# Own places for the last query and gate tiles of group two, a split store in the output pairs, and fewer steps at the end of group one's last descending scan tile

## The chip, the cores and the metric

The kernel runs on one core of one Trainium2 chip. A NeuronCore has five engines that run at the same time, each with its own queue of instructions that it takes in order: TensorE (PE, matrix multiplication; the loading of its weights is shown apart as PEld), VectorE (DVE), ScalarE (ACT), GpSimd (POOL) and SyncE (SP), which here does little but start DMA transfers. Engines wait for each other and for transfers by semaphores. The metric is the time of one execution on the device, in microseconds (us); lower is better. It is the median of several executions.

## The reference

One layer of a bidirectional encoder on two request groups with shared weights: 1024 rows of `x_sample` and 256 rows of `x_prompt`, 2048 features each. The layer adds to `x` the product of `w_out` with three groups of heads side by side, all computed from one projection of the normed rows:

```python
hn = rms_norm(x, norm_g)
proj = hn @ w_in
xbc, z_ssd, dt_raw, q, k, v, z_att, mq, z_mem = split_cols(proj, IN_SIZES)
xbc = silu(centred_dwconv(xbc, conv_w, conv_b))
...
y_f = ssd_scan(xs, dt[:, :, 0], A[0], Bm, Cm)                # over the rows, ascending
y_b = ssd_scan(reversed rows, dt[:, ::-1, 1], A[1], ...)     # and descending
yg = (y_f + y_b + d_skip * xs) * silu(z_ssd)
o_ssd = rms_norm(yg in two halves, ssd_norm_g)
o_att = window_attention(rms_norm(q), rms_norm(k), v, sink) * silu(z_att)
o_mem = softmax(rms_norm(mq) @ rms_norm(mk)) @ mv * silu(z_mem)
return x + concat([o_ssd, o_att, o_mem]) @ w_out
```

All of it is float32.

## The kernel before

**Rows and groups.** The 1280 rows are ten tiles of 128. Group one is tiles 0 to 4, group two tiles 5 to 9 (`base` is 0 or 5). Each float32 factor is kept as two parts, a rounded one and the rest (`xH`, `xL` for the rows, `wh`, `wl` for the weights), and each product is three matmuls. ACT writes `wh` (L216) and DVE `wl` (L217) from a loaded weight tile `wraw`.

**Blocks.** The work is a row of weight blocks, one behind the other. `block_tok` takes 512 columns of weights over 16 feature chunks k and five row tiles into five PSUM banks of the tag `acc`; each k is 15 matmuls of 128x512. In the last step (k = 14 and 15 together) the five tiles are finished in turn, and each is evicted by a function: `ev_gate` (ACT takes the tanh at L318, DVE finishes the gate at L319, SP stores it at L320) for the blocks z0 and z1, `ev_raw` (ACT copies at L341, SP stores at L342) for q and mq. `block_feat` computes 256 features of 640 rows with matmuls of 128x320; its last step is 48 matmuls. For group two the order is kv, q, za0, za1, z0, z1, mq, zm0, zm1, and then four output blocks o of 512 columns of `w_out` each. These work on the rows of group one, whose results have been refilled into `xH` and `xL` by then.

**Places.** A tile pool hands out buffers by tag. The evictions use the tags `evu` and `evt`, two buffers each, in turn: tile i takes `evt` for odd i and `evu` for even i, so the third `evu` tile of a block (i = 4) gets the buffer of the first (i = 0) once its store has landed. Only q of group one is different: its tiles 3 and 4 have places of their own (`tL7`, `tH7`). The tag `ch` has four buffers (`CH = 4`) of 128x640; it holds the chunks `chd` that `fill_direct` loads (L188) and splits into `xH` (L197, L200) and `xL` (L198, L201). `refill_o` (L1531) makes such refills during zm1 (at k = 3 and 7) and during the first output block (at k = 1 and 5): the attention outputs, the memory outputs and the two scan outputs `oT` become the rows that the output blocks multiply. Before it does, `need` runs the lane's steps until the tiles that it loads are finished.

**Lanes.** Attention, memory attention and the scan are generators in two queues (lane 0 and lane 1). After each k of a block, `pump` adds a rate to what each lane is owed and runs as many steps as are owed; a step runs a generator to its next `yield`. For group two the rates of lane 1 are 2.75 a feature block's two k's, that is 1.375 a k, in zm, and 2.4 a k in o. A feature block's last four k's come behind its last matmul. In `run`, a refill's `need` comes before the pump of the same k. The build puts each engine's instructions in order from such priorities and its own estimate of when operands are ready, so a load without operands can be issued long before its place in the program.

**The descending scan.** `ssd_down(t)` runs for t = 7 down to 0 in lane 1, then `ssd_up(8)`, `ssd_up(9)`, `ssd_down(9)`, `ssd_down(8)`. Each tile adds its parts, multiplies by the gate, and takes the sum of squares (L1146); POOL makes the factor `yrs` (L1157). `norm_ssd` (DVE, L1074) scales the two halves, and `turn_ssd(g)` turns half g: POOL sets a word (`yw`, L1082), PE transposes into `pr` (L647), ACT copies to `so` (L1088), SP stores to `oT` (L1089). A tile's norm and turns are done in the steps of the next tile; the last tile of a run (t = 0 or 8, `first`) does its own, after some empty steps. `ssd_up` starts with loads (`rf`, `rb`, L922) and has among its steps `xf` (L950), `fh` (L952) and the matmul `pst` (L937).

**The output of group two** comes in eight pairs (`block_pair`, with Strassen-like products over seven PSUM tiles p = 1, 2, 6, 5, 3, 7, 4 in that order, 3 matmuls of 128x320 for each p and k). `ev_pair` adds the seven products into two row blocks `r0` and `r1` (two halves of 320 each) and a helper `w`, all adds on DVE at L1240, and stores them: `r0` whole at L1256, the halves of `r1` at L1259 and L1262.

## Time and profile before

| what | value |
|---|---|
| time, median of 3 executions | 1773.84 us (1771.46 to 1775.32) |
| the profiled execution's own time | 1773.66 us |
| its span, first to last instruction | 1772.0 us |
| PE busy | 1762.2 us, 99% of the span, 11044 matmuls |
| DVE, ACT, POOL busy | 70%, 51%, 31% |
| bytes moved by DMA | 301.16 MB, mean 170 GB/s |
| stores of q, z, mq tiles of group two | 927 to 932, 1071 to 1077, 1149 to 1155, 1221 to 1227 us |
| first output block | from 1311.66 us |
| output pairs | from 1570.76 us |

A row of a timeline has the start in us from the span's start, the duration, the engine (a small q behind it marks its instruction queue, which issues DMAs), the line, the operation, the output and inputs by the program's names, the shape and the count; in square brackets stands how long the engine had been idle, and what ended it. A wait row has who waited, for whom, the total in us, the times and the longest. A row of windows has the stretch, its length, each engine's busy time and count, the granted clock of PE, the share of DMA time and GB/s.

### The profile page before, as it was taken

The page shows a single profiled execution, that of the slowest core. Times are in us where ns is not written, and L with a number is a line of the kernel's source. Part 1 is how long each engine was busy: PE and PEld are TensorE (multiplying, and loading weights), DVE is VectorE, ACT ScalarE, POOL GpSimd, SP SyncE. Part 2 cuts the span into 40 slices and gives each one's busy share as a digit, 9 for nine tenths or more (in the row PEclk, how much of TensorE's full clock was granted, in tenths as well). Part 3 has the DMA queues.
Part 4 walks back from the last instruction along what each step waited for, and adds up shares of the span by engine and source line. Part 5 has one row for each costly group of instructions (what it writes and reads, how often), then busy time and mean ns, then how long its engine had stood idle before and what let it go on. Part 6 is the DMA issues. An engine that isn't in the chain of part 4 may idle for free. (4 is left out here: it accounts for less than half of the span.)

```text
span 1772.0 us, 31942 instructions
## 1 busy us (share of the span) xinstructions
PE 1762.2 (99%) x11044; PEld 1608.4 (91%) x11044; DVE 1246.0 (70%) x2351; ACT 901.6 (51%) x2010; POOL 555.6 (31%) x980
## 2 busy tenths in 40 slices
PE   9999999999999999999999999999999999999999
PEld 7889999999998999999889988888988888899999
DVE  5596788888868878878665676566776654766665
ACT  6555455554434756656454555544446533543332
POOL 0105899998810100001001000011110000058775
PEclk9999999999999999999999999999999999999999
DMA  9654444445446645454545645557777755744442
GB/s 308 189 182 130 136 151 146 144 140 169 124 140 209 197 134 151 140 153 122 186 121 173 201 149 161 172 161 249 225 246 226 257 188 148 218 142 148 145 144 77
DMA packets 208210, 301.16 MB, mean 170 GB/s; under 512 B 19568, under 2 KB 86192, under 8 KB 208048
## 3 DMA queue, kind: packets, MB, share of 16 engines
q1 hardware_dynamic: 207904, 299.06, 54.1%
q8 instruction: 87, 1.43, 0.3%
q14 instruction: 75, 0.61, 0.1%
q10 hardware_dynamic: 144, 0.06, 0.0%
HBM read 236.36 MB, written 62.69 MB: 169 GB/s over the span
## 5 line engine op out<-in xcount | busy, mean ns | idle before, releaser
L217 DVE TENSOR_TENSOR wl<-wraw,wh 128x512 fp32r<-128x512 f32 (+1 forms) x480 | 346.4, 724 | 238.4 <-ACT wh L216 225.4
L216 ACT ACTIVATE wh<-wraw 128x512 fp32r<-128x512 f32 (+1 forms) x480 | 292.2, 613 | 301.6 <-PE acc L270 154.6
L268 PE MATMUL acc<-wh,xH 128*128 128x512 f32 (+1 forms) x1088 | 418.1, 385 | 0.0
L270 PE MATMUL acc<-wh,xL 128*128 128x512 f32 (+1 forms) x1088 | 410.4, 377 | 0.0
L269 PE MATMUL acc<-wl,xH 128*128 128x512 f32 (+1 forms) x1088 | 409.5, 376 | 0.0
L270 PEld LDWEIGHTS acc<-wh,xL 128*128 128x128 f32 x1088 | 204.2, 188 | 37.0 <-issue 0.2
L268 PEld LDWEIGHTS acc<-wh,xH 128*128 128x128 f32 x1088 | 204.3, 188 | 36.5 <-issue 2.7
L269 PEld LDWEIGHTS acc<-wl,xH 128*128 128x128 f32 x1088 | 204.5, 188 | 35.0 <-issue 1.2
L303 PE MATMUL acc<-xH,wh 128*128 128x320 f32 x640 | 203.0, 317 | 0.0
L305 PE MATMUL acc<-xH,wl 128*128 128x320 f32 x640 | 198.8, 311 | 0.0
L304 PE MATMUL acc<-xL,wh 128*128 128x320 f32 x640 | 198.5, 310 | 0.0
L216 ACT ACTIVATE sh<-ws 128x384 fp32r<-128x384 f32 x176 | 91.4, 523 | 204.8 <-POOL ws L1284 111.2
L217 DVE TENSOR_TENSOR sl<-ws,sh 128x384 fp32r<-128x384 f32 x176 | 124.4, 710 | 98.3 <-ACT sh L216 96.0
L1284 POOL TENSOR_TENSOR ws<-wraw 128x128 f32<-128x128 f32 x176 | 113.8, 646 | 202.4 <-DMA wraw<-in_w_in_pairs_dram 90.5
L303 PEld LDWEIGHTS acc<-xH,wh 128*128 128x128 f32 x640 | 120.1, 188 | 2.9 <-issue 2.4
L304 PEld LDWEIGHTS acc<-xL,wh 128*128 128x128 f32 x640 | 120.2, 188 | 1.7 <-issue 1.4
L305 PEld LDWEIGHTS acc<-xH,wl 128*128 128x128 f32 x640 | 120.2, 188 | 1.0 <-issue 0.9
L1284 POOL TENSOR_TENSOR ws<-wraw,ws 128x128 f32<-128x128 f32 x176 | 116.5, 662 | 13.8
L1284 POOL TENSOR_TENSOR ws<-ws,wraw 128x128 f32<-128x128 f32 x176 | 118.2, 671 | 0.0
L1284 POOL TENSOR_TENSOR wraw<-wraw 128x128 f32<-128x128 f32 x176 | 111.5, 633 | 13.7
L654 POOL MEMSET lgw<- 128x1 f32 x40 | 4.2, 105 | 312.0 <-DVE lg L718 161.6
L377 DVE SCALAR_TENSOR_TENSOR c<-u,vec,c 128x638 f32<-128x638 f32 (+1 forms) x96 | 90.0, 939 | 1.1 <-ACT c L372 0.4
(442 smaller groups left out, 3931.1 us busy)
## 6 DMA issues: line engine op xcount, KB each, us to landing
wraw<-in_w_in_laid_dram SPq DMA_DIRECT2D x176, 256.0 KB, 2.9
wraw<-in_w_in_pairs_dram SPq DMA_DIRECT2D x112, 256.0 KB, 2.7
wraw<-in_w_out_laid_dram SPq DMA_DIRECT2D x64, 256.0 KB, 3.6
wraw<-in_w_out_pairs_dram SPq DMA_DIRECT2D x64, 256.0 KB, 2.7
rf<-ac SPq DMA_DIRECT2D x40, 256.0 KB, 4.0
rb<-ac SPq DMA_DIRECT2D x40, 256.0 KB, 4.7
wraw<-in_w_mem_laid_dram SPq DMA_DIRECT2D x32, 256.0 KB, 4.3
xst<-in_x_sample_dram SPq DMA_DIRECT2D x20, 256.0 KB, 5.3
```

Of the source, the lines that this page charges most:

```text
L216: a = A.activation(h, raw, AF.Copy)
L217: b = V.tensor_sub(l, raw, h.bitcast(F32))
L268: T.matmul(ps[t][:, :n], sh, h[:, :n], start=(k_ == 0), stop=False)
L269: T.matmul(ps[t][:, :n], sh, l[:, :n], start=False, stop=False)
L270: T.matmul(ps[t][:, :n], sl, h[:, :n], start=False, stop=(k_ == KT - 1))
L303: T.matmul(o, sh, cur["H", q][:, m, c], start=(k == 0), stop=False)
L304: T.matmul(o, sh, cur["L", q][:, m, c], start=False, stop=False)
L305: T.matmul(o, sl, cur["H", q][:, m, c], start=False, stop=(k == KT - 1))
L377: V.scalar_tensor_tensor(out=c[0], in0=u[:, k:k + n], scalar=cw[k], in1=c[0], op0=ALU.mult, op1=ALU.add)
L654: G.memset(w.bitcast(F32)[(slice(None),) + tuple(slice(n - 1, n) for n in shape)], 0.0)
L1284: G.tensor_tensor(out=o, in0=x, in1=y, op=op)
```

## The change

- `out_place` now chooses the buffer for `ev_gate` and `ev_raw`. In group two (`base` is 5), tiles 3 and 4 of q, z0, z1 and mq take a buffer of the tag `ch`. Group one is as before.
- `ssd_down(0)` alone has two empty steps in place of three ahead of its norm and none behind it but the norm's own, and turns both halves in one step.
- `ev_pair` stores the first half of `r0` when product 2 is in, and the second half at product 3; the addition of `w` to `r1` is done in halves, the first at product 6 and the second at product 5.

```diff
@@ -312,9 +312,17 @@
             evac(1, ps[1])
 
 
+    def out_place(i, base, name):
+
+        if i > 2 and base == 0 and name == "qs":
+            return fin.tile([P, 512], F32, tag="tH7" if i == 4 else "tL7", name=name)
+        if i > 2 and base:
+            return rp.tile([P, 640], F32, tag="ch", name=name, bufs=CH)[:, :512]
+        return ev.tile([P, 512], F32, tag="evt" if i % 2 else "evu", name=name)
+
     def ev_gate(c, base):
         def f(i, ps):
-            z = ev.tile([P, 512], F32, tag="evt" if i % 2 else "evu", name="zs")
+            z = out_place(i, base, "zs")
             A.activation(z, ps, AF.Tanh, scale=0.5)
             V.scalar_tensor_tensor(out=z, in0=z, scalar=1.0, in1=ps, op0=ALU.add, op1=ALU.mult)
             S.dma_start(z_d[c][base + i], z)
@@ -334,10 +342,7 @@
 
     def ev_raw(dst, base):
         def f(i, ps):
-            if base == 0 and i > 2:
-                z = fin.tile([P, 512], F32, tag="tH7" if i == 4 else "tL7", name="qs")
-            else:
-                z = ev.tile([P, 512], F32, tag="evt" if i % 2 else "evu", name="qs")
+            z = out_place(i, base, "qs")
             last_raw[0] = A.activation(z, ps, AF.Copy).ins
             S.dma_start(dst[base + i], z)
         return f
@@ -1158,14 +1163,16 @@
         last_y["y"] = t, [x[0] for x in ld], rs
         yield
         if first:
-            for _ in range(3):
+            for _ in range(2 if t == 0 else 3):
                 yield
             norm_ssd()
             yield
-            yield
+            if t:
+                yield
             for g in range(2):
                 turn_ssd(g)
-                yield
+                if t or g:
+                    yield
 
 
 
@@ -1245,15 +1252,17 @@
                 add(r0[:, 0], ps, r0[:, 0])
             elif p == 2:
                 add(r0[:, 0], ps, r0[:, 0])
+                S.dma_start(y_turned[rows_[0], :320], r0[:, 0])
             elif p == 6:
                 add(w[:, 0], ps, w[:, 0])
+                add(r1[:, 0], w[:, 0], r1[:, 0])
             elif p == 5:
                 add(w[:, 1], ps, w[:, 0])
                 add(r0[:, 1], w[:, 1], r0[:, 1])
-                add(r1, w, r1)
+                add(r1[:, 1], w[:, 1], r1[:, 1])
             elif p == 3:
                 add(r0[:, 1], ps, r0[:, 1])
-                S.dma_start(hv(y_turned[rows_[0], :], 2), r0)
+                S.dma_start(y_turned[rows_[0], 320:], r0[:, 1])
             elif p == 7:
                 add(r1, ps.unsqueeze(1).broadcast_to([P, 2, 320]), r1)
                 S.dma_start(y_turned[rows_[1], 320:], r1[:, 1])
```

## The prediction, made before the changed kernel ran

> **What bounds the kernel now.** I read the page's head and busy shares, then the waits of TensorE (PE), then the stretches in which the edited lines run.

> ```profile
> span 1772.0 us, 31942 instructions
> PE 1762.2 (99%) x11044; PEld 1608.4 (91%) x11044; DVE 1246.0 (70%) x2351; ACT 901.6 (51%) x2010; POOL 555.6 (31%) x980
> PEclk9999999999999999999999999999999999999999
> ```

> PE is busy in 99% of the span, at a granted clock of 0.9 or more in every slice. The change takes no matmul away, so it can win only where PE stands still, or behind its last matmul. The waits of PE (who, for whom, total us, times, longest):

> ```profile
> PE warm L1592 <- DVE zero L1590: 1.3, 1, 1.3
> PE pst L937 <- ACT fh L952: 1.1, 1, 1.1
> PE pmt L647 <- DVE mpr L827: 1.1, 1, 1.1
> PE ppt L647 <- ACT pT L734: 1.0, 1, 1.0
> PE pmo L850 <- ACT mpT L839: 0.8, 1, 0.8
> PE pr L647 <- ACT so L1088: 0.4, 1, 0.4
> PE acc L1318 <- DVE wl L217: 0.3, 1, 0.3
> ```

> They are 6.0 us in all. Two of the seven lie where the change works: `ppt` behind `pT` and `pst` behind `fh`.

> **Part one, own places for tiles 3 and 4.** Before, tile 4 takes the buffer that tile 0 used, so its eviction waits for tile 0's store. How much of that is real stands in the wait shares of the two eviction lines (`qs`, then `zs`) and in the timelines of ACT and PE:

> ```profile
>   DMA mq<-qs: 1.1, 1
>   DMA z<-zs: 0.4, 1
> 1225.51 0.63 ACT L216 ACTIVATE wh<-wraw 128x512 fp32r<-128x512 f32 x1
> 1227.20 0.60 ACT L341 ACTIVATE qs<-acc 128x512 f32<-128x512 f32 x1 [1.06 <-DMA mq<-qs]
> 1228.12 0.65 PE L647 MATMUL ppt<-identr,lgw 128*128 128x128 f32 x4 [0.95 <-ACT pT L734]
> ```

> One eviction waited in the edited blocks: the last of group two's `mq`. (The `zs` wait of 0.4 is in group one's `z1`, which keeps its places.) ACT was free at 1226.14 and stood until 1227.20 with `pT` behind it, and PE stood 0.95 us for `pT`. With a place of its own the eviction starts 1.06 sooner and PE's 0.95 goes: **-0.95**, or 0 if `wh` is put ahead of `pT`.

> The places themselves cost something. All four `ch` buffers are in use there: the first four `chd` loads of the refill that `zm1` calls for are issued in advance, and their data is taken 236 us later.

> ```profile
> 1047.10 1.27 SPq L188 DMA_DIRECT2D chd<-oT  x3
> 1052.10 0.43 SPq L188 DMA_DIRECT2D chd<-oT  x1
> 1283.22 1.35 ACT L197 ACTIVATE xH<-chd 128x640 fp32r<-128x640 f32 x2
> 1220.00:1250.00 30.00, 29.05 (x204) 25.49 (x203) 20.74 (x42) 13.03 (x34) 7.14 (x18) 1.00 0.92 293
> L1116 SPq DMA_DIRECT2D ydT<-yd x1: 657/657/657, 1239.3 to 1239.3; - x1
> DMA to landing us min/median/max: 5.0/5.0/5.0
> 1244.41 0.51 PE L1122 MATMUL pd<-identr,ydT 128*128 128x128 f32 x4
> ```

> Buffers of one tag go out in program order, so the tiles of z0, z1 and `mq`, which stand ahead of the refill in the program, now get theirs first. The four loads (128x640 f32, 1.31 MB) then go once `mq`'s fifth tile has its place and its stores have landed: near 1227 to 1233. That is the fullest stretch for DMA in the group: in 1220 to 1250 its share is 0.92 (last columns: clock, DMA share, GB/s). At 293/0.92 = 318 GB/s the four take 4.1 us. Until 1239 there is about 1 us of room (0.08 of 12), so what is issued then lands up to 3.2 later. The `ydT` load of 1239.3 lands at 1244.3, and PE transposes it at 1244.41, with 0.1 to spare: PE would stand up to 3.2 there. The price is 0 to **+3.2**. I take +1.5, the middle: two buffers are free at once and their loads may land before the crowd, the other two come with the `yt` loads. The cover that makes it 0 is that SP holds the loads back past 1240; they are due only at 1283.

> **Part two, the shorter end of `ssd_down(0)`.** In lane steps: four pumps stand behind `zm1`'s last matmul (4 x 1.375 = 5.5 steps) and one behind k=0 of the first output block (2.4), so 7 or 8 steps are done before k=1 calls `need`. They begin with the step that turns tile 1's first half. Before, the turns of tile 0 are steps 9 and 10, so `need` forces them behind k=1. After, the norm is step 6 and both turns step 7: they are issued behind k=0.

> ```profile
> 1311.66 0.46 PE L268 MATMUL acc<-wh,xH 128*128 128x512 f32 x1
> 1315.17 0.39 PE L268 MATMUL acc<-wh,xH 128*128 128x512 f32 x1
> 1318.58 0.80 PE L647 MATMUL pr<-identr,yw 128*128 128x128 f32 x8
> 1316.36 0.88 DVE L1074 TENSOR_SCALAR yd<-yd,yrs 128x512 f32<-128x512 f32 x2 [2.16 <-POOL yrs L1157]
> 1316.96 0.49 POOL L1082 MEMSET yw<- 128x1 f32 x2 [0.64 <-DVE yd L1074]
> 1319.97 4.54 DMA oT<-so
> 1322.03 0.78 SPq L922 DMA_DIRECT2D rf<-ac  x1
> 1324.53 1.75 SPq L188 DMA_DIRECT2D chd<-oT  x4
> 1330.79 0.83 ACT L200 ACTIVATE xH<-chd,vec 128x640 fp32r<-128x640 f32 x1 [1.29 <-DMA chd<-oT]
> 1334.10 0.63 ACT L952 ACTIVATE fh<-xf 128x512 fp32r<-128x512 f32 x1 [0.52 <-DVE xf L950]
> 1334.78 0.50 PE L937 MATMUL pst<-fh,bth 128*128 128x512 f32 x1 [1.09 <-ACT fh L952]
> ```

> One chain: the transposes (1318.58) let ACT copy, the store goes at 1319.97 and lands 4.54 later, then the `chd` loads go, ACT stands 1.29 us for the second with `fh` queued behind, and PE stands 1.09 for `fh`. If the transposes come sooner, their words must be ready: POOL's second memset ends at 1317.45, 2.28 us behind k=0's end (1315.17), ten matmuls of 0.23 into k=1. I put them there, 1.1 us sooner than now, since lane work stands elsewhere too where its operands are ready. Store and loads follow 1.1 sooner; SP is free for the loads from 1322.81 on, so 1.7 is the most. ACT's stall shrinks to 0.2, `fh` comes 1.1 sooner, and the 1.09 goes: **-1.1**. The other end is +1.2 (PE stands 2.28 and the 1.09 goes). I take the low end because of PE's seven waits one, of 0.4, is at such transposes. The steps saved move nothing else: `need` had forced them anyway.

> **Part three, `ev_pair`.** Per pair one DMA more (a 320 KB store as two of 160) and one DVE add more (a 128x640 as two 128x320). Only the last pair's tail is bare.

> ```profile
> L1240 DVE TENSOR_TENSOR yr<-yu,yr 128x640 f32<-128x640 f32 x8 | 6.8, 851 | 0.0
> L1240 DVE TENSOR_TENSOR yr<-yu,yr 128x320 f32<-128x320 f32 x8 | 4.0, 500 | 0.3
> 1765.75 0.49 DVE L1240 TENSOR_TENSOR yu<-acc,yu 128x320 f32<-128x320 f32 x1 [0.39 <-PE acc L1318]
> 1766.27 1.23 DVE L1240 TENSOR_TENSOR yr<-yu,yr 128x320 f32<-128x320 f32 x2
> 1767.42 0.48 DVE L1240 TENSOR_TENSOR yr<-acc,yr 128x320 f32<-128x320 f32 x1
> 1767.82 1.41 DVE L1240 TENSOR_TENSOR yr<-accm,yr 128x640 f32<-128x640 f32 x2
> DMA to landing us min/median/max: 1.8/2.9/3.1
> ```

> From 1765.75 to 1769.23 DVE hardly pauses, so it and not PE sets the last store. The half of `r1` that moves ahead falls into the 0.39 that DVE stood before; at 0.50 it overshoots by 0.11. Behind it stays 0.45 in place of about 0.70 (the records overlap: two that take 1.23 let the next start after 1.15). So **-0.15**, between -0.3 and +0.1. The sooner half store is worth 0: the last store's 1.8 us to landing is already the least of its line's eight. At the seven joints before, the same pause covers the added work; if each paid 0.15 it would be 1.0 us. SP has nothing due where the new store stands.

> [...]

> **Sum.** -0.95 + 1.5 - 1.1 - 0.15 = -0.7 on the profiled execution's 1773.66 (span 1772.0 and 1.66 around it): 1773.0. The median of the runs, 1773.84, is 0.18 above that execution.

> **The rivals.**
> - *The `chd` loads cost nothing*: held back or swallowed. 1773.66 - 0.95 - 1.1 - 0.15 = 1771.5. For it: 50 us of room until they are due. Against it: at 1047 such loads went as soon as they could.
> - *They cost all of it* (slower): PE stands 3.2 at `pd`: 1774.7. It decides from 2.2 us on. For it: 0.1 us to spare there. Against it: the order of `ydT` and the loads on SP isn't known.
> - *The transposes stand ahead of their words*: behind k=0 PE stands 2.28. With the rest as forecast and `fh`'s wait gone, 1773.0 + 2.3 = 1775.3. For it: DVE already stands 2.16 for `yrs`. Against it: how rare such waits are.
> - *The waits move on* to the next queued work: only the tail is left, 1773.5, inside the forecast's spread.

> **How the numbers follow.** Forecast (1772.3 to 1774.2, with the last rival) 0.42; no cost 0.30; all of it 0.15; transposes ahead 0.13. About 0.2% (3.5 us) is what a measurement of this kernel tells from no change; the three runs differ by as much. Faster by more (below 1770.3): 0.2, two thirds of the no-cost case, if a new order of the lanes also spares 1.2 of PE's other waits. Slower by more (above 1777.4): 0.07, the second and third rival together. Within: 0.73. The range, 1770.0 to 1775.8, holds all four cases but a part of those two ends.

> **What would show it.** Right: no idle before `mq`'s fifth `qs` and no PE wait on `pT` near 1228; the four `chd` loads near 1230 in place of 1047, and a PE wait on `ydT` near 1244; the eight `pr` inside k=1, no PE wait on `fh`; DVE's tail 0.15 shorter. Wrong: `chd` loads still at 1047 or only after 1240, a PE wait at `pr` on `yw`, ACT idle on `chd` as before, or new PE waits elsewhere between 930 and 1500.

## The result: 1774.86 us, slower by 0.14%

| | before | changed |
|---|---|---|
| median, 22 executions each | 1772.89 us | 1774.86 us |
| lowest to highest | 1770.06 to 1775.32 | 1773.07 to 1777.79 |
| ratio | | 1.0014 (1.0008 to 1.0019) |
| profiled execution: own time, span | 1773.66, 1772.0 | 1776.04, 1774.3 |

The forecast was 1773.0, from 0.7 us gained; 2.0 us were lost. The ratio with its 95% interval is an estimate from all executions of both kernels and not the quotient of the two medians, which is 1.0011 here; in the experiments below the two lie up to 0.0006, or 1 us, apart. The longer series show something else: before has a median of 1772.3 to 1772.9 in every one of them, so the profiled execution on which the sum was made (1773.66) was itself about 1 us late.

From the changed kernel's page and the waits of PE:

```profile
span 1774.3 us, 31950 instructions
PE 1764.4 (99%) x11044; PEld 1609.9 (91%) x11044; DVE 1248.7 (70%) x2359; ACT 902.1 (51%) x2010; POOL 555.9 (31%) x980
PE pxs L935 <- ACT mpr L826: 2.3, 1, 2.3
PE warm L1601 <- DVE zero L1599: 1.3, 1, 1.3
PE pr L652 <- DVE yd L1079: 1.0, 1, 1.0
PE pd L1127 <- DMA ydT<-yd: 0.4, 1, 0.4
```

(From `ev_raw` to the scan, line numbers are 5 higher than before; behind that, up to 9.) The two waits that were to go, `ppt` for `pT` and `pst` for `fh`, are gone. A longer one stands in their place: `pxs`, 2.3 us for `mpr`. PE is also busy 2.2 us longer for the same 11044 matmuls.

**Where the 2.3 us come from.** The timelines of PE, POOL, SP, ACT and DVE over the start of the output block:

```profile
1310.53 0.46 PE L268 MATMUL acc<-wh,xH 128*128 128x512 f32 x1
1315.83 0.49 POOL L1087 MEMSET yw<- 128x1 f32 x2 [0.64 <-DVE yd L1079]
1315.85 0.86 PE L652 MATMUL pr<-identr,yw 128*128 128x128 f32 x8 [0.97 <-DVE yd L1079]
1317.02 1.20 SPq L1094 DMA_DIRECT2D oT<-so  x2
1321.32 1.74 SPq L188 DMA_DIRECT2D chd<-oT  x4
1320.16 0.58 ACT L801 ACTIVATE mqh<-pmq 128x512 fp32r<-128x512 f32 x1
1326.09 0.83 ACT L200 ACTIVATE xH<-chd,vec 128x640 fp32r<-128x640 f32 x1 [5.35 <-DMA chd<-oT]
1327.35 2.25 ACT L200 ACTIVATE xH<-chd,vec 128x640 fp32r<-128x640 f32 x3
1329.51 0.55 ACT L826 ACTIVATE mpr<-pms,mm,mr 128x256 f32<-128x256 f32 x1
1326.95 0.88 DVE L201 SCALAR_TENSOR_TENSOR xL<-chd,vec,xH 128x640 fp32r<-128x640 f32 x1 [5.37 <-ACT xH L200]
1327.76 0.68 DVE L820 TENSOR_REDUCE mm<-pms 128x2 f32<-128x512 f32 x1
1330.74 0.72 PE L935 MATMUL pxs<-identr,xc 128*128 128x128 f32 x4 [2.34 <-ACT mpr L826]
```

Read it as a queue, not as a list of times. ACT ends `mqh` at 1320.74, and the next instruction in its queue is now the fill `xH`, whose `chd` has only been asked for at 1321.32. It stands 5.35 us. Behind it wait the exponentials `mpr` of the memory scores. DVE does the same with `xL`, and the row maxima `mm` behind it are inputs of those exponentials. PE needs a PSUM tile that the exponentials read and stops for 2.34 us. Before the change, DVE took the maxima and ACT the exponentials ahead of the first fill:

```profile
1324.58 0.68 DVE L815 TENSOR_REDUCE mm<-pms 128x2 f32<-128x512 f32 x1
1325.78 0.57 ACT L821 ACTIVATE mpr<-pms,mm,mr 128x256 f32<-128x256 f32 x1 [1.84 <-DVE mm L817]
1328.65 0.83 ACT L200 ACTIVATE xH<-chd,vec 128x640 fp32r<-128x640 f32 x1 [0.31 <-DMA chd<-oT]
```

The `chd` loads do go 3.2 us sooner (1324.53 before). Presumably that is why the build put the fills first: by its own estimate the data would be there. The estimate itself stands in no trace.

**What the stop costs besides.** Windows of the changed kernel (a row has the busy times of PE, its weight load, DVE, ACT and POOL, then the granted clock, the share of DMA time and GB/s):

```profile
1328.00:1330.70 2.70, 0.41 (x2) 0.00 (x0) 2.70 (x7) 2.70 (x8) 0.00 (x0) 1.00 0.68 219
1330.70:1334.20 3.50, 3.46 (x14) 2.87 (x15) 3.50 (x14) 2.96 (x8) 0.20 (x2) 0.52 0.91 306
```

For 3.5 us behind the stop the granted clock is 0.52, and PE does 14 matmuls; part two alone, with the clock at 1.00, does 20 in as long. Together: the first output matmul comes 1.13 us sooner than before (1311.66), the last two DVE adds 2.37 us later (1770.19 against 1767.82). From that first matmul to the first of the output pairs (1573.39, 1570.76 before) PE takes 3.76 us longer, and the rows account for nearly all of it: 0.97 for `yd`, 2.34 at `pxs` and about 1.4 by the half clock, less the 1.09 that PE no longer stands for `fh`, make 3.6.

### The profile page after: what moved, and what is told of

Its sections match the earlier page's. It is cut to its first block, busy times and chain, and to the rows that moved or that the text cites. A ratio compares the mean times of both kernels' runs of the same rounds, so it can differ in the third digit from the quotient of the medians.

```text
span 1774.3 us, 31950 instructions
## 1 busy us (share of the span) xinstructions
PE 1764.4 (99%) x11044; PEld 1609.9 (91%) x11044; DVE 1248.7 (70%) x2359; ACT 902.1 (51%) x2010; POOL 555.9 (31%) x980
## 4 chain that ended last, share of the span: by engine, by line
PE 96%; DMA 1%; DVE 1%; ACT 0%; issue 0%; SPq 0%; POOL 0%; DVEq 0%; ACTq 0%
PE acc L268 13%; PE acc L269 13%; PE acc L270 13%; PE acc L1327 7%; PE acc L1325 7%; PE acc L1326 7%; PE acc L303 5%; PE acc L305 5%; PE acc L304 5%; PE accm L1326 3%; PE accm L1325 3%; PE accm L1327 3%; PE po L749 1%; PE py L1019 1%; PE ppt L652 1%; PE pmo L855 1%
## 5 line engine op out<-in xcount | busy, mean ns | idle before, releaser
L217 DVE TENSOR_TENSOR wl<-wraw,wh 128x512 fp32r<-128x512 f32 (+1 forms) x480 | 348.2, 727 | 242.7 <-ACT wh L216 227.9
L216 ACT ACTIVATE wh<-wraw 128x512 fp32r<-128x512 f32 (+1 forms) x480 | 292.4, 614 | 305.1 <-PE acc L270 161.1
L268 PE MATMUL acc<-wh,xH 128*128 128x512 f32 (+1 forms) x1088 | 418.6, 385 | 0.0
L268 PEld LDWEIGHTS acc<-wh,xH 128*128 128x128 f32 x1088 | 204.7, 188 | 36.6 <-issue 2.7
L216 ACT ACTIVATE sh<-ws 128x384 fp32r<-128x384 f32 x176 | 91.4, 523 | 205.2 <-POOL ws L1293 103.2
L217 DVE TENSOR_TENSOR sl<-ws,sh 128x384 fp32r<-128x384 f32 x176 | 123.0, 702 | 94.4 <-ACT sh L216 93.1
```

Of the source, the lines that this page charges most:

```text
L216: a = A.activation(h, raw, AF.Copy)
L217: b = V.tensor_sub(l, raw, h.bitcast(F32))
L268: T.matmul(ps[t][:, :n], sh, h[:, :n], start=(k_ == 0), stop=False)
```

## The experiments

**Each part alone.** The first three runs apply one part of the diff to the kernel before, and the fourth is the full change with one edge of order more:

```diff
-            A.activation(h, ch, AF.Copy, scale=gain)
+            with ExitStack() as st:
+                if last_exp[0] is not None:
+                    st.enter_context(tc.issue_after(last_exp[0]))
+                A.activation(h, ch, AF.Copy, scale=gain)
```

(The main part of it; `last_exp[0]` is the last exponential that `mem_attn` has issued.)

*Part one* (`out_place`):

> Part one alone (own places for tiles 3 and 4). Theory Q (the two engine queues: part two put the fills of the refill, which wait for the chd loads, ahead of the exponentials of the memory scores on ScalarE and of the row maxima on VectorE; that, not the places, is the loss): 1.0 to 1.2 us less than before, ratio about 0.9994; TensorE's wait for pT is gone and its wait for ydT is below 0.6 us; the waits for fh (1.1) and at pmt (1.1) stand as before. Rival P (the chd loads that moved into the full stretch are the loss): 1.5 to 2 us more than before, ratio 1.001, with waits at pd and later transposes.

Measured: 1772.16 against 1772.26, ratio 0.9994 (0.9986 to 1.0003). Its waits of PE, and a window:

```profile
PE pst L942 <- ACT fh L957: 2.3, 1, 2.3
PE pd L1127 <- DMA ydT<-yd: 0.4, 1, 0.4
1334.30:1337.20 2.90, 2.87 (x7) 2.25 (x8) 2.67 (x6) 2.71 (x5) 0.00 (x0) 0.50 0.84 239
```

`pT` and `ydT` are as expected, and rival P's 1.5 us lie outside the interval. Two waits that this part doesn't touch didn't stand as before: `pmt` is 0.4 in place of 1.1, and `fh` is 2.3 in place of 1.1, with half the clock behind it: such a wait belongs to an execution as much as to a kernel.

*Part two* (the yields of `ssd_down(0)`):

> Part two alone (sooner store in the last block). Theory Q: 3.3 to 3.9 us more than before, ratio about 1.002; ScalarE stands over 5 us for a chd load near 1326 with the exponentials behind it, TensorE stands 2.3 us for mpr at pxs near 1331 and its granted clock then falls to about 0.5 for some 3.5 us; TensorE stands 1.0 us for yd at the transposes. Rival P: within 0.3 us of before. Rival W (the transposes ahead of their words are the loss): about 1.0 us more, less the 1.1 of the wait for fh, so no difference.

Measured: 1776.60 against 1772.26, ratio 1.0020 (1.0012 to 1.0029), 3.5 us lost.

```profile
PE pxs L930 <- ACT mpr L821: 2.3, 1, 2.3
PE pr L647 <- DVE yd L1074: 1.0, 1, 1.0
1331.30:1334.80 3.50, 3.42 (x20) 2.91 (x21) 3.50 (x14) 3.50 (x9) 0.20 (x2) 1.00 0.89 313
```

By its middle value this part alone loses more than the whole change, though the intervals overlap. The stop is the same, but the clock stayed at 1.00 behind it; that half of the expectation missed.

*Part three* (`ev_pair`):

> Part three alone (the end of the last descending scan tile). Theory Q: 0.3 us less than before, ratio 0.9998, all of it behind TensorE's last matmul; nothing moves ahead of it. Rival E (each joint pays for its added addition and store): 0.5 to 1.0 us more, seen as new waits at the joints before the last.

Measured: 1771.90 against 1772.26, ratio 0.9996 (0.9988 to 1.0004). The timeline of DVE at the end, and one row of before:

```profile
1762.94 0.49 DVE L1240 TENSOR_TENSOR yu<-acc,yu 128x320 f32<-128x320 f32 x1 [0.20 <-PE acc L1320]
1763.47 0.49 DVE L1240 TENSOR_TENSOR yr<-yu,yr 128x320 f32<-128x320 f32 x1
1763.88 0.48 DVE L1240 TENSOR_TENSOR yu<-acc,yu 128x320 f32<-128x320 f32 x1
1764.40 0.89 DVE L1240 TENSOR_TENSOR yr<-yu,yr 128x320 f32<-128x320 f32 x2
1765.61 1.41 DVE L1240 TENSOR_TENSOR yr<-accm,yr 128x640 f32<-128x640 f32 x2
```

```profile
1764.87 0.49 DVE L1240 TENSOR_TENSOR yu<-acc,yu 128x320 f32<-128x320 f32 x1 [0.20 <-PE acc L1318]
```

From the `yu` add of product 5 to the last two adds are 1.73 us (1763.88 to 1765.61); before it was 2.07 (1765.75 to 1767.82), 0.34 more. But the half add that moved ahead makes product 5's add a little late: it comes 0.94 behind product 6's add here (1762.94 to 1763.88) and 0.88 before (1764.87 to 1765.75). From product 6's add the tail is 0.28 shorter (2.67 against 2.95). PE shows no new wait at the joints, so by the rows rival E is out.

*The full change with the fills behind the exponentials*:

> The full change, with one order added: ScalarE's copy of a fill is issued behind the last exponential of the memory scores that stands ahead of it in the program. Theory Q: the loads stay where the change put them (issued near 1321.3), ScalarE takes the exponentials first, TensorE's 2.3 us wait at pxs and the half clock behind it are gone; of part two only the 1.0 us wait for yd stays, against the 1.1 for fh that goes; 1.0 to 1.8 us less than before, ratio about 0.9992, and 3 to 4 us less than the changed kernel. Rival P: still 1 us or more above before. Rival W: about as before.

Measured: 1771.89 against 1772.26, ratio 0.9996 (0.9988 to 1.0005). ACT, SP and PE of this kernel:

```profile
1321.93 1.74 SPq L189 DMA_DIRECT2D chd<-oT  x4
1326.75 0.56 ACT L830 ACTIVATE mpr<-pms,mm,mr 128x256 f32<-128x256 f32 x1 [1.84 <-DVE mm L826]
1329.19 1.56 ACT L204 ACTIVATE xH<-chd,vec 128x640 fp32r<-128x640 f32 x2
1334.10 0.63 ACT L962 ACTIVATE fh<-xf 128x512 fp32r<-128x512 f32 x1 [0.52 <-DVE xf L960]
PE pr L656 <- DVE yd L1084: 1.0, 1, 1.0
```

Counted from the block's first matmul (1311.36 here, 1310.53 there), the loads are as early as in the changed kernel, 10.57 against 10.79 us; only the old order is back, and the wait at `pxs` and ACT's stall in front of the exponentials are gone. The wait for `fh` is gone too, but not because `fh` is sooner: it starts 22.74 us behind the block's first matmul, against 22.44 before. PE comes to it later, since it has stood 0.98 us for `yd`. The ratios 0.9996 and 1.0014 put 3.2 us between the two kernels, measured each against its own series of before. This shows the cause of the loss: the place of the fills in ACT's queue. The gain over before is smaller than expected and its interval holds 1.

**How much the removed waits were worth.** Parts one and three without part two:

> Parts one and three without part two. Theory Q (the fills in front of the exponentials are the loss, the other two parts gain a little): 1.0 to 1.6 us less than before, ratio about 0.9993, and 3 to 4 us less than the changed kernel. Rival P (the moved chd loads cost more than they bring): no less than before. By the three profiles in which the lines of the waits for pT and fh are unchanged, these waits are 0.2 to 1.1 and 0.6 to 2.3 us, so a single profile of this kernel may lie 1.5 us to either side.

Measured: 1772.29 against 1772.48, ratio 0.9998 (0.9989 to 1.0006): less than Q's 1.0 to 1.6, though its interval takes that in, so P isn't decided by this run. From the changed kernel it is 2.8 us by the ratios, a little less than the 3 to 4 expected. A second profile of before was taken beside it:

> The kernel before once more, for a second profile of it. If the waits for pT (1.0) and fh (1.1) belong to the kernel, they stand here within 0.2 of that; if they come from when the stores happen to land, they differ by half a microsecond or more, as they do in the profiles whose edits are elsewhere.

Its waits of PE; its own time was 1772.15:

```profile
PE pst L937 <- ACT fh L952: 0.7, 1, 0.7
PE ppt L647 <- DVE yd L1123: 0.4, 1, 0.4
```

The wait for `pT` isn't there at all: `ppt` stands 0.4 for something else. The wait for `fh` is 0.4 shorter, between the two expectations. In the five profiles without part one, `ppt` waits 1.0, 0.4, 1.1, 0.2 and (in the run without places below) 1.3 us, 0.8 in the mean. The wait for `fh`, in the five profiles with neither an earlier store nor a new order, is 1.1, 0.7, 2.3, 0.6 and 0.8, 1.1 in the mean. ACT's stall for the store `mq<-qs`, from which the first comes, is 1.06 us in the first profile of before, 0.49 in the second and 1.36 in the run without places; each of the three ended with the landing of that store.

**Data that are there.**

> The full change, but the refill of the scan's first half reads rows that were written long before (oT_d[0] in place of oT_d[2]; those four rows of the refill's input are left out). The fills stay ahead of the exponentials in the program. Theory Q: it is the landing of the data, behind the order, that ScalarE and VectorE stand for; with data there they do not stand, pxs does not wait and the granted clock stays full: 1.0 to 2.2 us less than before, 3 to 4 less than the changed kernel. Rival O (the order alone, four fills of 0.83 us ahead of the exponentials, makes them late): still 1 us or more above before.

Measured: 1776.60 against 1772.48, ratio 1.0021 (1.0012 to 1.0030). It didn't do what it was for: the fills of the refill's second half, still of `oT_d[3]`, moved up to the free place.

```profile
1330.12 0.83 ACT L200 ACTIVATE xH<-chd,vec 128x640 fp32r<-128x640 f32 x1 [5.04 <-DMA chd<-oT]
1332.09 0.75 PE L935 MATMUL pxs<-identr,xc 128*128 128x128 f32 x4 [3.83 <-ACT mpr L826]
1332.00:1335.50 3.50, 3.41 (x11) 2.83 (x12) 2.93 (x11) 2.83 (x8) 0.20 (x2) 0.50 0.96 343
```

One fill, not four, stood ahead of the exponentials here, and PE's stop at `pxs` was longer still. (PE also stood 2.0 us at `pr` for `so`, so the total has more than one cause.) With both halves read from data that are there:

> As the run with data that are there, but both halves of the scan's refill read oT_d[0] (eight rows of the refill's input are left out), since in that run the fills of the second half, which still waited for the store, took the place ahead of the exponentials. Theory Q: ScalarE stands for no chd load near 1326, no wait at pxs: 0.5 to 2.0 us less than before and 2.5 us or more less than the changed kernel beside it. Rival O (the place of the store and of the turns costs it, not the fills): still 1 us or more above before.

Measured: 1773.22 against 1772.33, ratio 1.0009 (1.0000 to 1.0018).

```profile
PE pr L652 <- ACT so L1093: 1.6, 2, 1.2
PE pr L652 <- DVE yd L1079: 0.9, 1, 0.9
```

The wait at `pxs` is gone, as theory Q had it; the total isn't below before, so its number missed, and rival O's 1 us or more is the nearer (1.6 by the ratio). The fills now stand ahead of the copies `so` of earlier tiles, and PE waits there. The run moved too much to separate order from landing. The fourth run shows that the order is needed for the loss; whether the order alone would cost anything with the data there stays open.

**A version with the turns in their time.** Parts one and three, the fills behind the exponentials, and instead of part two's yields a call in the middle of k=1:

```diff
             for t in range(nt):
+                if mid is not None and k == 1 and t == 3:
+                    mid()
```

(The main part of it; for the first output block, `mid` calls `need(ssd_down, range(5))`.)

> Parts one and three, the fills behind the exponentials, and in place of part two's steps the rest of the scan's lane called after nine of the fifteen matmuls of k=1, so that the eight transposes stand six matmuls (1.4 us) behind the place that the change gave them. Theory Q: no wait for yd (it was 1.0 us), the store 0.4 us later than in the changed kernel and still early enough that neither ScalarE nor the wait for fh stands: 2.0 to 2.7 us less than before, ratio about 0.9987. Rival V (the gains are of waits that vary from run to run, and the next late operand takes most of each): within 1 us of before.

Measured: 1771.03 against 1772.48, ratio 0.9991 (0.9983 to 1.0000). The timelines of PE, SP and ACT:

```profile
1315.92 0.80 PE L658 MATMUL pr<-identr,yw 128*128 128x128 f32 x8
1322.92 1.74 SPq L189 DMA_DIRECT2D chd<-oT  x4
1326.97 1.56 ACT L204 ACTIVATE xH<-chd,vec 128x640 fp32r<-128x640 f32 x2
1332.28 0.46 PE L949 MATMUL pst<-fh,bth 128*128 128x512 f32 x1
```

No bracket stands behind the transposes, the first fills or `pst`: none waits. Here `fh` does come sooner: it starts at 1331.33, 20.96 us behind the block's first matmul (1310.37), which is 1.5 less than before; in the second profile of this kernel it is 21.42, 1.0 less. That is what part two was meant for. Once more, beside the same without part one, and the changed kernel:

> The kernel with the turns in the middle of k=1 once more, for its interval: it was 0.9991 (0.9983 to 1.0000). Theory Q: 0.9985 to 0.9994 of before, and 2.5 to 5 us less than the changed kernel beside it. Rival V (the gains were of waits that vary by chance): 0.9994 to 1.0003.

> The same without part one: the places as before, the last part, the fills behind the exponentials, the turns in the middle of k=1. If part one is worth the 0.5 to 1.1 us that its own profile shows, this is that much slower than the kernel with the places beside it, about 0.9995 of before; if the wait for pT comes and goes by chance and the moved loads take the rest, the two differ by less than 0.5 us.

> The changed kernel again, beside the others on one chip: 2.0 to 3.0 us more than before (it was 1.0014, 1.0008 to 1.0019); the wait at pxs for mpr is 2.2 to 2.4 us again, since it follows from the order of the queues. Whether the granted clock falls behind it is open: it fell in the changed kernel's profile (0.52 for 3.5 us), not in that of part two alone, with a stop of the same length.

| run (before beside them: 1772.33) | median | ratio |
|---|---|---|
| turns in the middle, again | 1771.13 | 0.9994 (0.9985 to 1.0003) |
| the same without part one | 1771.44 | 0.9996 (0.9987 to 1.0004) |
| the changed kernel, again | 1775.69 | 1.0017 (1.0008 to 1.0026) |

The version with the turns in the middle is 4.6 us below the changed kernel beside it, and the mean of its two ratios is 0.99925, 1.3 us below before; by intervals of 0.0009 each the mean is uncertain by about 0.0006, so it beats before, by little. Between theory Q (2.0 to 2.7 at first) and rival V it lies in the middle. What part one adds to it is 0.3 us by the medians, not to be told from nothing and inside the 0.5 that was expected if the wait comes and goes, though the profile without it shows the whole wait for `pT`, 1.3 us.

A window of the changed kernel's second profile:

```profile
1332.50:1336.00 3.50, 3.42 (x14) 2.83 (x15) 3.50 (x14) 3.50 (x9) 0.20 (x2) 0.55 0.86 300
```

The wait at `pxs` is there in each of the three profiles with part two and the refills as they were written (2.3, 2.3, 2.8), a little above what was expected in the last.

## Why the prediction was wrong

The time, 1774.86, lay inside the range; the sign of the sum was wrong, through one term. That it fell between the times of the two slower rivals (1774.7 and 1775.3) is chance: PE stood 0.4 us at `pd` and not 3.2, and 0.97 at the transposes and not 2.28.

- **Part two, -1.1 forecast, +3.5 (2.1 to 5.1) measured: the step that failed.** It said that "ACT's stall shrinks to 0.2, `fh` comes 1.1 sooner", and further: "The steps saved move nothing else". The store and the loads did move, by 3.0 and 3.2 us, 1.1 of it because the block starts sooner. But ACT's stall grew from 1.29 to 5.35 us. The step took the order of ACT's and DVE's queues from the trace of before. The order is made anew when the steps move: the fills went ahead of the exponentials, and a stall that had `fh` behind it became a stall with the exponentials behind it. That the build orders each engine by its own estimate of when operands are ready was known; the question "what is queued behind the fill now?" was asked only for the old order. None of the rivals had it. With the order held and the turns behind their words, as in the version with the turns in the middle, the step's own account comes true: `fh` is 1.0 to 1.5 us sooner and PE doesn't wait for it.
- **The transposes ahead of their words**, a rival priced at 2.28 us with a chance of 0.13, came true at 0.97. The words were not sooner: POOL begins them 5.30 us behind the block's first matmul in both kernels (1316.96 - 1311.66, 1315.83 - 1310.53). But the transposes stand behind 18 matmuls, three into k=1, and they start with the first word, while the price reckoned from the end of k=0 to the end of the second. By itself it cancels against the wait for `fh`, as the kernel with the fills behind the exponentials shows.
- **Part one, -0.95 + 1.5 forecast, about -0.95 by the rows.** The places did what they say (a fifth `qs` without a wait), and three of the four `chd` loads moved to where the prediction put them, the fourth to 1245.26:

```profile
1226.04 0.60 ACT L346 ACTIVATE qs<-acc 128x512 f32<-128x512 f32 x1
1231.99 0.55 SPq L188 DMA_DIRECT2D chd<-oT  x1
1233.56 0.90 SPq L188 DMA_DIRECT2D chd<-oT  x2
1245.26 0.61 SPq L188 DMA_DIRECT2D chd<-oT  x1
```

  Their price was over-estimated: PE stands 0.4 us at `pd`, not 1.5, and the later wait for `so` (0.4 before) isn't listed in this profile, which would give that back: -0.95 + 0.4 - 0.4. The timed run alone says -1.0 (-2.5 to +0.5) by its ratio and -0.1 by its medians, so its worth in time isn't shown.
- **Part three, -0.15 forecast, -0.28 by the rows**, inside the bounds of -0.3 and +0.1. The half add overshoots DVE's pause before product 5 by 0.06 us, not 0.11, and what stays behind it is 0.34 shorter.
- **The base.** Two of the waits that were to be won came from one execution that was 1 us late. By the means over five profiles they are worth 0.8 and 1.1; the one profile gave 0.95 and 1.1. That is near, but a sum made against 1773.66 had to start from 1772.5.

## What to carry to other kernels

When a change moves work earlier in a program whose queues are ordered by a planner, ask of every engine that consumes it what will now stand behind the consumer, and pin the consumer behind the critical work if its data may be late. In the changed kernel the early place of one fill in ACT's queue became a stall of 5.35 us for everything behind it. A wait of 1 us in one profile should be looked up in a second profile of the same kernel before it is counted as a gain.

## What the runs showed of the hardware

A stop of PE of 2.3 to 3.8 us was followed by half the granted clock in four profiles of five: the changed kernel's two, the run with the places alone, and the first run with data that are there (0.52, 0.55, 0.50 and 0.50 in the windows above); behind the 2.3 us of part two alone it stayed at 1.00. That is about 1.4 us on top of the stop: 14 matmuls in 3.5 us against the 20 of part two's window, with the same eight transposes in both, so six matmuls fewer at 0.23 us each. Behind the 1.09 us that PE stood for `fh` in the kernel before, the windows show 1.00.

```profile
1327.40:1330.82 3.42, 1.08 (x6) 0.58 (x4) 3.42 (x8) 3.42 (x9) 0.00 (x0) 1.00 0.69 231
1330.82:1334.23 3.41, 3.41 (x14) 2.82 (x15) 3.41 (x14) 2.87 (x8) 0.20 (x2) 0.50 0.90 299
1327.05:1330.47 3.42, 2.07 (x10) 1.38 (x8) 2.87 (x6) 3.42 (x6) 0.00 (x0) 1.00 0.61 173
1330.47:1333.88 3.41, 2.50 (x16) 2.14 (x17) 3.41 (x13) 3.41 (x11) 0.10 (x1) 1.00 0.99 360
```

In the changed kernel the stop falls into one cell, PE is busy for 1.08 us of it, and the next cell has half the clock. In part two alone an edge divides a stop of the same length, PE is busy for 2.07 and 2.50 us of the two cells, and the clock stays. The cells ahead of the other three slow stretches have 0.65 us busy (the changed kernel's second profile), 0.95 (the first run with data that are there) and 1.49 (the places alone). In the traces of the two kernels the least busy cell with full clock behind it has 1.63 us (from 1766.72 in the kernel before); the last cell of each, at the end of the program, has none, and half the clock stands behind it. So in the cells named here it was where the stop fell on the grid, and not its length alone: behind 1.49 us busy and less came half the clock, behind 1.63 and more full clock. What comes behind a cell between the two is not shown.
